# Moving fill units, first transposes and weight splits in a two-branch attention block

## The chip, the cores and the metric

The kernel runs on one core of a Trainium2 chip. The metric is device time in microseconds (us), as the median of several executions. The profile is of one further execution. TensorE is PE in the rows, VectorE DVE, ScalarE ACT, GpSimd POOL, SyncE SP.

## What is computed

One decoder block for 512 tokens of width 1024, in float32. All that matters here is this, cut from the reference:

```python
h = rms_norm(x, norm_g[layer])
proj = h @ w_in[layer]
fq, fk, fv, fz, mq, mk, mv, mz, ga, gb, fl = split_cols(proj, IN_SPLITS)
# fox: 8 heads of 64, causal, with a forget bias; q and k are RMS-normalised
y_fox = from_heads(fox_attention(q, k, v, log_f)) * jax.nn.silu(fz)
# moba: 8 heads of 64; q and k are RMS-normalised and rotated (partial_rope)
y_moba = from_heads(moba_attention(q, k, v)) * jax.nn.silu(mz)
merged = (jax.nn.sigmoid(ga + b_gate[layer, 0]) * (y_fox @ w_fox[layer])
          + jax.nn.sigmoid(gb + b_gate[layer, 1]) * (y_moba @ w_moba[layer]))
x = x + merged @ w_out[layer]
```

At 512 tokens and blocks of 256, every block is selected, so moba is computed as causal attention as well.

## The kernel before

**Precision.** A float32 operand is split in a high part (a ScalarE copy) and a low part (a VectorE subtraction), and a product is three matmuls: high by high, high by low, low by high. A weight chunk is 128 x 4 x 256 numbers; `split` (L131 to L137) makes its two parts, named wh and wl, with four buffers each.

**Fill units.** A name such as fkb is 256 columns of the input projection: branch f or m, then q, k, v or z, then half a or b. Its weights come in two chunks. `unit(name, t)` computes 128 tokens of it, 24 matmuls into a bank of the tag pj (two banks), and evicts it. For q and k each second unit normalises two token tiles: a square sq on ScalarE, a reduction on VectorE, a power and a product on GpSimd, and for branch m four rotation steps on GpSimd (`norm_qk`, `do_rope`). sq has the tag u, which it shares with ysh. v is split in two parts and kept. The units of wf0 to wf3 multiply fox's result by w_fox; the target of the first eviction, f03, has the tag v with two buffers, and so comes after v_mva.

**Attention groups.** There are four groups: fox a, fox b, moba a, moba b, of four heads each. A group consists of steps. Tr(0), Tr(1) transpose q and k of a pair of heads into p_qT and p_kT, split them, and copy KH to the other 64 partitions by a DMA. Aa(h) computes logits lg and exponentials. Bb(h) transposes the exponentials through three banks p_a, p_b, p_cc, splits them (pth, ptl) and multiplies by v into the only bank pv; ScalarE copies half of it (ysh) and VectorE adds. Yp(pair) scales. p_qT, p_kT, p_a, p_b, p_cc and p_ri share the tag tp with three banks. A group's body is Aa(0), Aa(1), Tr(1), Bb(0), Aa(2), Bb(1), Yp(0), Aa(3), with the previous group's Yp(1) put behind Aa(0); its tail is Bb(2), Bb(3). Tr(0) of the next group is the step `following`.

**Order.** `inter` (L1023) deals the steps of a group and the units of its fill alternately into one program order, in proportion to their numbers. The fill of group 0 is fkb, fqb, fvb, of group 1 mka, mqa, mva, of group 2 mkb, mqb, mvb, of group 3 wf0 to wf3. From the program order a planner makes a fixed order for each engine ahead of the run: by its own estimates of time it issues, on each engine, the instruction that is ready and stands earliest in program order. So TensorE's matmuls of steps and of units are mixed finely, and a unit can run far ahead of its place. Buffers of one tag are given out in program order.

**Splits.** Every fill unit first calls `pump(i)` (L179): it makes the splits up to piece i + 3 and, as raw buffers come free (four), has SP load further chunks. i is the first piece of the unit's own name (two less for wf), so the first unit of a name has both pieces of the next name split. In the first two groups two units of each fill also carry `make_sums`, six VectorE instructions and two ScalarE copies, with stores.

Of the kernel before, what the change touches and what calls it, by code (L numbers as in the profile page):

```python
# [25 lines left out]
C_NG, C_BG, C_FQ, C_FK, C_MQ, C_MK, C_BF, C_GQ, C_GK, C_END = 0, 8, 24, 25, 26, 27, 28, 36, 52, 68  # L26
# [3 lines left out]
def fox_moba_kernel(ctx: ExitStack, tc, xT, x, w_in, w_fl, w_fox, w_moba, w_out, cst, rope, out):  # L30
# [3 lines left out]
    V, A, G, T = nc.vector, nc.scalar, nc.gpsimd, nc.tensor  # L34
# [56 lines left out]
    def col(c, n=1):  # L91
        return cs[:, c:c + n]
# [13 lines left out]
    for i in range(WARM):  # L106
# [8 lines left out]
                    fill=NEG, base=0, channel_multiplier=1)  # L115
# [60 lines left out]
    loads, preps, first_prep = [], [], {}  # L176
    done = {"loads": 0, "preps": 0}

    def pump(i):  # L179

        while True:
            j = done["loads"]
            if j < len(loads) and (j < WR or loads[j - WR][1] < done["preps"]):
                loads[j][0]()
                done["loads"] += 1
            elif done["preps"] < len(preps) and done["preps"] <= i + 3:
                preps[done["preps"]]()
                done["preps"] += 1
            else:
                return  # L190
# [65 lines left out]
    def make_sums(k):  # L256
        def tl(tag, dt=F32):
            return t2("y", 15, f"sum_{tag}", dt=dt)
        a, b = XT[k], XT[k + 4]
        out = []  # L260
        f0, f1 = tl("sf"), tl("sf")
        s3, s2, s1, s4 = f0[:, 0:HT], f0[:, HT:S], f1[:, 0:HT], f1[:, HT:S]
        for o, x, y, op in ((s3, a[:, 0:HT], a[:, HT:S], OP.subtract), (s1, a[:, HT:S], b[:, HT:S], OP.add),
                            (s2, s1, a[:, 0:HT], OP.subtract), (s4, b[:, 0:HT], s2, OP.subtract)):
            V.tensor_tensor(out=o, in0=x, in1=y, op=op)
        for i, f in enumerate((f0, f1)):
            hl = [tl("sh", F32R), tl("sl", F32R)]
            A.activation(hl[0], f, AF.Copy)
            V.tensor_tensor(out=hl[1], in0=f, in1=hl[0].bitcast(F32), op=OP.subtract)
            out.extend((d[2 * i:2 * i + 2, :, k, :].rearrange("s p t -> p s t"),  # L270
                        t.bitcast(F32).rearrange("p (s t) -> p s t", t=HT)) for d, t in zip(S_dram, hl))

        def store():
            for d, t in out:
                A.dma_start(out=d, in_=t)
        return store
# [71 lines left out]
    def rope_tables():  # L348
        nc.sync.dma_start(out=rp, in_=rope)
        for nm, c in (("mq", C_GQ), ("mk", C_GK)):  # L350
            tab = con.tile([P, NT, 32], F32, name=f"tab_{nm}")
            g = col(c, 16)
            G.tensor_tensor(out=tab[:, :, 0:16], in0=rp[:, :, 0:16],
                            in1=g[:, None, :].to_broadcast([P, NT, 16]), op=OP.mult)
            G.tensor_tensor(out=tab[:, :, 16:24], in0=rp[:, :, 16:24],
                            in1=g[:, None, 8:16].to_broadcast([P, NT, 8]), op=OP.mult)
            G.tensor_tensor(out=tab[:, :, 24:32], in0=rp[:, :, 24:32],
                            in1=g[:, None, 0:8].to_broadcast([P, NT, 8]), op=OP.mult)
            CA[nm] = tab
# [27 lines left out]
    def unit(name, t):  # L387
        def go():
            p = pj(f"pj_{name}{t}")
            unit_mm(p, name, t)  # L390
            if name[1] == "v":
                evac_v(p, name, t)
            else:
                evac_qk(p, name, t)
        return go
# [17 lines left out]
    def unit_z(name, c):  # L413
        def go():
            p = (tp if name == "fzb" else pj)(f"pz_{name}{c}")
            tr_mm(p, name, c)
            z = t2("y", 15, f"zs_{name}{c}")
            s = t2("u", 4, "sg")
            V.tensor_tensor(out=z, in0=p, in1=rbc, op=OP.mult)
            A.activation(s, z, AF.Tanh, scale=0.5)  # L420
            V.scalar_tensor_tensor(z, s, 1.0, z, op0=OP.add, op1=OP.mult)
            ZS["f", 2 * (name[2] == "b") + c] = z
        return go
# [67 lines left out]
    def moba_begin():  # L491
        for o in range(2):
            rows = slice(HD, HD + 32) if o == 0 else slice(0, 32)
            for tl in KLt[o]:
                G.memset(tl[rows, :].bitcast(F32), 0.0)
# [178 lines left out]
    def unit_f(i, c):  # L674
        def go():
            j = 2 * i + c
            p = pj(f"pf{j}")
            br_mm(p, f"wf{i}", "f", c)
            if j == 0:
                f = sb.tile([P, 4, S], F32, name="f03", tag="v", bufs=2)  # L680
                FS[0], FS[1] = f[:, 0:2, :], f[:, 2:4, :]
            elif j in (4, 6):
                FS[j // 2] = sb.tile([P, 2, S], F32, name=f"f{j}", tag="qk", bufs=4)
            A.activation(FS[i][:, c, :], p, AF.Copy)  # L684
        return go
# [134 lines left out]
    def merge_a(i, c):  # L820
        if True:
            j = 2 * i + c
            p = pj(f"pm{j}")
            br_mm(p, f"wm{i}", "m", c)
            u = SG[i][:, c, :]
            V.tensor_tensor(out=u, in0=p, in1=u, op=OP.mult)
            if i % 2:
                V.tensor_tensor(out=u, in0=u, in1=FS[i][:, c, :], op=OP.add)
            else:
                G.dma_start(out=u, in_=FS[i][:, c, :], accum_op=OP.add)  # L830
# [166 lines left out]
    def units(name):  # L997
        k = name[:2]
        if k[0] == "G":
            return groups[name]  # L1000
        if k == "wf":
            return [unit_f(int(name[2]), c) for c in range(2)]
        if k == "wm":
            i = int(name[2])
            return [lambda c=c: merge_a(i, c) for c in range(2)]
        if k[1] == "z":
            return [unit_z(name, c) for c in range(2)]
        return [unit(name, t) for t in range(4)]

    def filler(names):  # L1010
        res = []
        for nm in names:
            for n, u in enumerate(units(nm)):
                def go(i=first_prep[nm] + (n if nm[0] == "G" else -2 if nm[:2] == "wf" else 0), u=u):
                    pump(i)
                    u()
                res.append(go)
        return res

    def last_on(engine):  # L1020
        return next(i for i in reversed(nc.cur_bb.bb.instructions) if i.engine == engine)

    def inter(a, b):  # L1023
        n, m = len(a), len(b)
        ia = ib = 0
        while ia < n or ib < m:
            if ib >= m or (ia < n and ia * m <= ib * n):
                a[ia]()
                ia += 1
            else:  # L1030
                b[ib]()
                ib += 1

    def seq(names):
        for u in filler(names):
            u()
# [14 lines left out]
    norm_row()  # L1051
    pump(0)
    fz = filler(["fza", "fzb"])
    for k, u in enumerate(fz):
        u()
        if k < 3:
# [3 lines left out]
    enter("attention")  # L1060
    zero_kl()
    rope_tables()
    plan = (("f", "a", C_FQ, C_FK, ["fkb", "fqb", "fvb"]),
            ("f", "b", C_FQ, C_FK, ["mka", "mqa", "mva"]),
            ("m", "a", C_MQ, C_MK, ["mkb", "mqb", "mvb"]),
            ("m", "b", C_MQ, C_MK, ["wf0", "wf1", "wf2", "wf3"]))
    head, body, tail, gate = attn_group("f", "a", col(C_FQ), col(C_FK))
    head[0]()
    for n in range(4):
        nxt = []  # L1070

        def following(n=n, nxt=nxt):
            br, half, cq, ck = plan[n + 1][:4]
            if n == 1:
                moba_begin()
            nxt.extend(attn_group(br, half, col(cq), col(ck)))
            nxt[0][0]()
        fill = filler(plan[n][4])
        if n < 2:
            for k, at in ((2 * n, 2), (2 * n + 1, 6)):  # L1080
                store = []

                def with_sums(u=fill[at], k=k, store=store):
                    u()
                    with tc.issue_after(last_on(mybir.EngineType.DVE)):
                        store.append(make_sums(k))

                def with_store(u=fill[at + 1], store=store):
                    u()
                    store[0]()  # L1090
                fill[at], fill[at + 1] = with_sums, with_store
        inter(body + ([following] if n < 3 else []) + tail, fill)
        if n < 3:
            body, tail = nxt[1][:1] + gate + nxt[1][1:], nxt[2]
            gate = nxt[3]
# [138 lines left out]
```

## Time and profile before

| What | Value |
|---|---|
| median of 3 runs | 431.78 us (431.44 to 433.05) |
| profiled execution | 433.64 us |
| its span | 431.9 us |
| mean granted clock of its span | 0.994 |
| TensorE busy | 419.5 us |
| VectorE busy | 337.5 us |

A row of a timeline gives the start in us from the start of the span, the duration, the engine, the line, the operation, output and inputs, and the count; in brackets stands the time for which the engine had been idle before it, and what ended that. Ends of matmuls are modelled, so the starts are the better measure of TensorE's pace. In the table by stretch, PEclk is the granted clock of TensorE as a share of full speed.

### The profile page before, as it was taken

How to read it: one execution, taken by the hardware profiler on the slowest of the kernel's cores; microseconds unless marked ns; L12 is line 12 of the kernel's file. 1: busy time of each engine (PE TensorE's matmuls, PEld its weight loads, DVE VectorE, ACT ScalarE, POOL GpSimd, SP SyncE). 2: the span in 40 equal slices, each digit the busy share in tenths (PEclk: the TensorE clock that was granted, in tenths of full speed). 3: DMA queues.
4: the chain of work that ended last, by engine and by line, in shares of the span. 5: the costliest groups of instructions: out<-in, count | busy, mean ns of one | idle time of the engine just before them, and what ended most of it. 6: DMA issues, size and time to landing. Idle time of an engine off the chain costs nothing.

```text
span 431.9 us, 7832 instructions
## 1 busy us (share of the span) xinstructions
PE 419.5 (97%) x2956; PEld 391.5 (91%) x2956; DVE 337.5 (78%) x571; ACT 272.4 (63%) x521; POOL 111.2 (26%) x127
## 2 busy tenths in 40 slices
PE   7999999999989989999997999999999999999996
PEld 6998899999989979999985789999999989988884
DVE  4669976887959978697669766599998685789973
ACT  4985436867658575697657766437757534686450
POOL 1048200224204766018630105044000011022140
PEclk9999999999999999999999999999999999999999
DMA  7981235253452444331231104915050835796484
GB/s 241 396 293 58 69 127 150 68 187 118 129 145 87 129 130 137 122 123 40 95 106 43 26 24 179 361 71 178 21 194 2 271 71 116 239 261 116 98 142 152
DMA packets 26374, 59.53 MB, mean 138 GB/s; under 512 B 3168, under 2 KB 7968, under 8 KB 26336
## 3 DMA queue, kind: packets, MB, share of 16 engines
q1 hardware_dynamic: 13552, 38.38, 26.8%
q0 software_dynamic: 3968, 9.44, 9.9%
q10 hardware_dynamic: 8816, 11.21, 8.7%
q8 instruction: 23, 0.38, 0.4%
q14 instruction: 15, 0.12, 0.1%
HBM read 48.37 MB, written 6.32 MB: 127 GB/s over the span
## 4 chain that ended last, share of the span: by engine, by line
PE 59%; DVE 6%; issue 1%; DMA 1%; ACT 1%; ACTq 0%; DVEq 0%
PE pb_GB L748 3%; PE pb_GA L748 3%; PE pb_GA L745 3%; PE pb_GB L747 3%; PE pb_GB L745 3%; PE pb_GA L747 3%; PE po L948 3%; PE po L946 3%; PE po L947 3%; PE pm L671 2%; PE pm L672 2%; PE pm L670 2%; PE pf L670 2%; PE pb_GZ L747 2%; PE pb_GZ L748 2%; PE pb_GZ L745 2%
## 5 line engine op out<-in xcount | busy, mean ns | idle before, releaser
L334 POOL TENSOR_TENSOR ff<-ss,mh 128x8 f32<-128x8 f32 x16 | 30.5, 1914 | 59.8 <-DVE ss L332 59.4
L564 ACT ACTIVATE p<-p,negm 128x128 f32<-128x128 f32 (+1 forms) x64 | 35.7, 560 | 14.8 <-DVE negm L562 12.2
L562 DVE CUSTOM_DVE_ANT_0 p<-lg,mask 128x128 f32<-128x128 f32 (+1 forms) x64 | 30.9, 488 | 14.8 <-PE lg L560 14.1
L134 ACT ACTIVATE wh_GB<-wr_gb 128x1024 fp32r<-128x1024 f32 x14 | 14.6, 1058 | 13.9 <-PE pm L671 5.9
L559 PE MATMUL lg<-KH,QS 128*128 128x128 f32 (+1 forms) x64 | 20.8, 334 | 2.2 <-DMA KH<-KH 2.1
L136 DVE TENSOR_TENSOR wl_GA<-wr_ga,wh_GA 128x1024 fp32r<-128x1024 f32 x14 | 19.9, 1445 | 1.6 <-ACT wh_GA L134 1.6
L908 ACT ACTIVATE wh_o<-wr_o 128x1024 fp32r<-128x1024 f32 x14 | 14.8, 1058 | 10.0 <-PE pb_GB L747 2.8
L136 DVE TENSOR_TENSOR wl_GB<-wr_gb,wh_GB 128x1024 fp32r<-128x1024 f32 x14 | 16.8, 1218 | 5.0 <-ACT wh_GB L134 5.0
L909 DVE TENSOR_TENSOR wl_o<-wr_o,wh_o 128x1024 fp32r<-128x1024 f32 x14 | 16.9, 1220 | 3.7 <-ACT wh_o L908 3.7
L134 ACT ACTIVATE wh_GA<-wr_ga 128x1024 fp32r<-128x1024 f32 x14 | 14.4, 1055 | 6.5 <-DVE wr_ga L706 3.4
L830 POOL DMA_DIRECT2D uGB<-f x4 | 3.5, 870 | 56.9 <-issue 47.0
L638 ACT ACTIVATE ysh<-pv 64x512 f32<-64x512 f32 x16 | 9.5, 592 | 11.3 <-PE pv L614 8.9
L532 ACT ACTIVATE QS<-p_qT,cs 64x512 fp32r<-64x512 f32 x16 | 10.9, 682 | 7.6 <-PE p_qT L523 4.0
L559 PEld LDWEIGHTS lg<-KH,QS 128*128 128x128 f32 x64 | 12.0, 189 | 3.4 <-DMA KH<-KH 2.6
L533 DVE SCALAR_TENSOR_TENSOR QS<-p_qT,cs,QS 64x512 fp32r<-64x512 f32 x16 | 12.0, 750 | 3.2 <-ACT QS L532 2.8
L670 PE MATMUL pf<-yhf,wh_wf 128*128 128x512 f32 x32 | 13.0, 407 | 0.8 <-ACT f L684 0.8
L748 PE MATMUL pb_GA<-Gh,wl_GA 128*128 128x256 f32 x48 | 13.5, 281 | 0.0
L748 PE MATMUL pb_GB<-Gh,wl_GB 128*128 128x256 f32 x48 | 13.5, 281 | 0.0
L747 PE MATMUL pb_GA<-Gl,wh_GA 128*128 128x256 f32 x48 | 13.5, 281 | 0.0
L745 PE MATMUL pb_GA<-Gh,wh_GA 128*128 128x256 f32 x48 | 13.5, 281 | 0.0
L609 ACT ACTIVATE pth<-p_a 128x512 fp32r<-128x512 f32 x16 | 9.5, 593 | 6.3 <-PE p_a L603 6.2
L745 PE MATMUL pb_GB<-Gh,wh_GB 128*128 128x256 f32 x48 | 13.5, 280 | 0.0
(485 smaller groups left out, 1840.8 us busy)
## 6 DMA issues: line engine op xcount, KB each, us to landing
wr_ga<-in_w_in_dram SPq DMA_DIRECT2D x8, 512.0 KB, 6.4
wr_gb<-in_w_in_dram SPq DMA_DIRECT2D x8, 512.0 KB, 4.8
wr_o<-in_w_out_dram SPq DMA_DIRECT2D x8, 512.0 KB, 11.6
xt<-in_xT_dram SPq DMA_DIRECT2D x8, 256.0 KB, 5.9
x<-in_x_dram SPq DMA_DIRECT2D x8, 256.0 KB, 6.7
KH<-KH ACTq DMA_DIRECT2D x16, 128.0 KB, 2.3
s_dramh<-sum_sh ACTq DMA_DIRECT2D x8, 256.0 KB
s_draml<-sum_sl ACTq DMA_DIRECT2D x8, 256.0 KB, 3.3
```

The source lines that it names most:

```text
L134: A.activation(hi[:, :, 0:n], src, AF.Copy)
L136: eng.tensor_tensor(out=lo[:, q, 0:n], in0=src[:, q], in1=hi[:, q, 0:n].bitcast(F32), op=OP.subtract)
L334: G.tensor_tensor(out=f2, in0=ss.rearrange("p t h -> p (t h)"), in1=mh, op=OP.pow)
L559: T.matmul(lg[:, :n], qs[:, qt], kh[:, :n], start=True, stop=False)
L562: V.tensor_tensor_reduce(pt, lg[:, :n], mask[:, 512 - n:512], -0.125, 3.0e38, op0=OP.add, op1=OP.min, accum_out=mkn[:, hh, i:i + 1])
L564: A.activation(pt, pt, AF.Exp, bias=mkn[:, hh, i:i + 1], scale=-1.0, accum_out=rs[:, hh, i:i + 1])
L670: T.matmul(p, hi[:, k, cc], yh, start=(k == 0), stop=False)
L745: T.matmul(o, hi[:, k, cc], lh, start=(n < 3 and c == 0 and k == 0), stop=False, skip_group_check=True)
L747: T.matmul(o, hi[:, k, cc], ll, start=False, stop=False, skip_group_check=True)
L748: T.matmul(o, lo[:, k, cc], lh, start=False, stop=(k == 3), skip_group_check=True)
L908: A.activation(wide(hi), wide(R[key, c]), AF.Copy)
L909: V.tensor_tensor(out=wide(lo), in0=wide(R[key, c]), in1=wide(hi).bitcast(F32), op=OP.subtract)
```

## The change

Three edits. The first two units of a q, k or v name call `pump` with a number lower by one, so that the first piece of the next name is split at the first unit and the second at the third; this takes in fva, ahead of the groups. The last two units of v (":23") go to the head of the next group's fill, ahead of its other units. Tr(0) of the next group stands behind Bb(2) instead of before it.

With the new counts `inter` deals as follows. Group 0: ..., Aa(3), fqb3, Bb(2), fvb0, Tr(0), fvb1, Bb(3). Groups 1 and 2: ..., Aa(3), q2, Bb(2), q3, Tr(0), v0, Bb(3), v1, where q3 is the last unit of mqa or mqb. Before, it was ..., q3, Aa(3), v0, Tr(0), v1, Bb(2), v2, Bb(3), v3 in all three. Group 3 has ten units instead of eight.

```diff
+    def ahead(nm, n):
+        return n if nm[0] == "G" else -2 if nm[:2] == "wf" else -1 if nm[1] in "qkv" and n < 2 else 0
+
     def filler(names):
         res = []
         for nm in names:
+            nm, _, part = nm.partition(":")
             for n, u in enumerate(units(nm)):
-                def go(i=first_prep[nm] + (n if nm[0] == "G" else -2 if nm[:2] == "wf" else 0), u=u):
+                def go(i=first_prep[nm] + ahead(nm, n), u=u):
                     pump(i)
                     u()
-                res.append(go)
+                if not part or str(n) in part:
+                    res.append(go)
         return res
...
-    plan = (("f", "a", C_FQ, C_FK, ["fkb", "fqb", "fvb"]),
-            ("f", "b", C_FQ, C_FK, ["mka", "mqa", "mva"]),
-            ("m", "a", C_MQ, C_MK, ["mkb", "mqb", "mvb"]),
-            ("m", "b", C_MQ, C_MK, ["wf0", "wf1", "wf2", "wf3"]))
+    plan = (("f", "a", C_FQ, C_FK, ["fkb", "fqb", "fvb:01"]),
+            ("f", "b", C_FQ, C_FK, ["fvb:23", "mka", "mqa", "mva:01"]),
+            ("m", "a", C_MQ, C_MK, ["mva:23", "mkb", "mqb", "mvb:01"]),
+            ("m", "b", C_MQ, C_MK, ["mvb:23", "wf0", "wf1", "wf2", "wf3"]))
...
-        inter(body + ([following] if n < 3 else []) + tail, fill)
+        inter(body + tail[:1] + ([following] if n < 3 else []) + tail[1:], fill)
```

## Rows read from the trace of the kernel before

**Rows 1.** The page's share table: busy us (share of the span) and instructions of each engine.

```profile
PE 419.5 (97%) x2956; PEld 391.5 (91%) x2956; DVE 337.5 (78%) x571; ACT 272.4 (63%) x521; POOL 111.2 (26%) x127
```

**Rows 2.** Busy time by stretch, core 0; columns in the first line, clock where PEclk stands.

```profile
core 0: us, PE busy (x) PEld busy (x) DVE busy (x) ACT busy (x) POOL busy (x), PEclk, DMA share, GB/s
120.00:135.00 15.00, 13.70 (x112) 13.18 (x111) 10.20 (x22) 9.59 (x22) 1.82 (x2) 1.00 0.44 115
150.00:165.00 15.00, 13.11 (x93) 12.67 (x92) 11.84 (x27) 10.10 (x24) 7.27 (x8) 0.89 0.46 138
...
225.00:240.00 15.00, 12.15 (x67) 9.46 (x66) 13.85 (x31) 12.29 (x29) 0.00 (x0) 1.00 0.25 71
268.00:432.00 164.00, 159.75 (x1093) 147.72 (x1091) 131.30 (x145) 90.95 (x128) 25.80 (x23) 0.99 0.55 155
```

**Rows 3.** Waits of PE: engine line waited for: us, times, longest.

```profile
PE pv L614 <- DVE ptl L610: 2.5, 2, 1.9
PE lg L559 <- DMA KH<-KH: 2.1, 2, 1.3
```

**Rows 4.** Timeline of PE, 157 to 161: start us, us, operation, idle before in brackets.

```profile
157.80 0.33 PE L613 MATMUL pv<-pth,v_fvb 128*128 128x384 f32 x1
160.02 0.55 PE L614 MATMUL pv<-ptl,v_fvb 128*128 128x384 f32 x1 [1.89 <-DVE ptl L610]
```

**Rows 5.** Timeline of DVE, 156 to 160: the two splits ahead of ptl.

```profile
156.41 1.21 DVE L136 TENSOR_TENSOR wl_mkb<-wr_mkb,wh_mkb 128x1024 fp32r<-128x1024 f32 x1
...
158.16 1.21 DVE L136 TENSOR_TENSOR wl_mkb<-wr_mkb,wh_mkb 128x1024 fp32r<-128x1024 f32 x1
159.29 0.68 DVE L610 TENSOR_TENSOR ptl<-p_b,pth 128x512 fp32r<-128x512 f32 x1
```

**Rows 6.** Timeline of PE, 214 to 224, transposes alone (matmuls between them left out).

```profile
214.09 0.38 PE L523 MATMUL p_qT<-ident,qn_mqb 128*128 128x128 f32 x2
...
214.75 0.60 PE L603 MATMUL p_a<-ident,p 128*128 128x128 f32 x4
...
219.21 0.60 PE L603 MATMUL p_b<-ident,p 128*128 128x128 f32 x4
...
223.24 0.38 PE L523 MATMUL p_qT<-ident,qn_mqb 128*128 128x128 f32 x2
...
223.63 0.38 PE L603 MATMUL p_cc<-ident,p 128*128 128x128 f32 x2
```

**Rows 7.** Timeline of PE, 227 to 239: the end of the third group's last head.

```profile
228.28 0.33 PE L559 MATMUL lg<-KH,QS 128*128 128x128 f32 x1 [0.75 <-DMA KH<-KH]
...
228.85 0.60 PE L603 MATMUL p_a<-ident,p 128*128 128x128 f32 x4
...
235.67 0.37 PE L614 MATMUL pv<-ptl,v_mva 128*128 128x256 f32 x1
...
238.06 0.50 PE L670 MATMUL pf<-yhf,wh_wf 128*128 128x512 f32 x1 [0.76 <-ACT f L684]
```

**Rows 8.** Timeline of ACT, 212 to 238: the square, the KH copy, the branch's eviction.

```profile
212.29 0.59 ACT L638 ACTIVATE ysh<-pv 64x512 f32<-64x512 f32 x1 [0.79 <-PE pv L614]
212.91 0.63 ACT L327 ACTIVATE sq<-qn_mqb 128x512 f32<-128x512 f32 x1
...
224.95 0.49 ACTq L536 DMA_DIRECT2D KH<-KH  x1
...
237.41 1.09 ACT L684 ACTIVATE f<-pf 128x512 f32<-128x512 f32 x2
```

**Rows 9.** Timeline of POOL, 215 to 220: last of the normalising and rotation of mqb.

```profile
219.03 0.46 POOL L372 TENSOR_TENSOR qn_mqb<-ra,rb 128x128 f32<-128x128 f32 x1
```

**Rows 10.** Timeline of PE, 99 to 102: first and last of eighteen projection matmuls.

```profile
99.09 0.28 PE L306 MATMUL pj_fvb<-wh_fvb,Gh 128*128 128x256 f32 x1
...
101.07 0.28 PE L308 MATMUL pj_fvb<-wh_fvb,Gl 128*128 128x256 f32 x1
```

**Rows 11.** Timeline of DVE, 212 to 214: the sum that frees the pv bank.

```profile
212.91 0.69 DVE L639 TENSOR_TENSOR yma<-pv,ysh 64x512 f32<-64x512 f32 x1 [1.18 <-ACT ysh L638]
```

## The prediction, as it was made

> **What bounds the kernel now.** I read the page's share table first: TensorE is busy 97% of the span, no other engine over 78% [rows 1]. So only TensorE's own gaps can be won. Then the table by stretch, for where they lie [rows 2]. From 268 us to the end 159.75 of 164 us are busy and what is missing lies after the last product, out of the change's reach. In the attention stage, three stretches of 15 us are short: 120 to 135 by 1.30 us, 150 to 165 by 1.89, 225 to 240 by 2.85. In 150 to 165 the granted clock is 0.89 as well; with its two levels 2.4 and 1.2 GHz that is 2 x 0.11 x 15 = 3.3 us at the lower one, of which half, 1.65 us, is lost. In the other two it is 1.00. The idle counts come short by what the modelled ends hide: at 157.80 a 384-column matmul is followed by the next start only 2.22 us later, while the row itself puts the idle at 1.89 [rows 4]; less some 0.18 us of issue for 384 columns (an estimate: the 18 projection matmuls of 256 columns start 0.1165 us apart [rows 10], times 1.5) 2.04 us are lost, 0.15 more per restart.
>
> Three different causes, then:
>
> - A, at 124 us: PE waits 1.30 us for the copy of KH [rows 3].
> - B, at 158 us: PE waits 1.89 us for ptl [rows 3, 4]. On VectorE two splits of one weight name, wl_mkb, 1.21 us each, were queued ahead of it, at 156.41 and 158.16 [rows 5].
> - C, 225 to 240 us: several short waits, 2.85 us. The row behind the last shows why there was no filler: pf waits for the eviction of an earlier pf [rows 7], which runs only at 237.41 [rows 8]. Its target f03 has the tag of the v tiles, so it needs the buffer of v_mva, and v_mva's last product stands at 235.67 [rows 7]. Two banks pj were full until then.
>
> Why was v_mva held so long? The transposes p_qT and p_kT of the next group take two of three tp banks at 214.09 and wait for the second half of q, which POOL finishes at 219.03 + 0.46 = 219.5 [rows 6, 9]; the second half of p_qT is at 223.24 [rows 6]. Head 2 has one bank in that time: p_a at 214.75, p_b at 219.21, p_cc at 223.63 [rows 6]. Head 3 begins at 228.85 [rows 7].
>
> **The change, part by part.** No instruction is added or removed. The fill units keep their order among themselves; what moves is their place against the attention steps, the order of Tr(0) and Bb(2), and the place of the splits with the loads that follow them on SP's queue.
>
> *Tr(0) behind Bb(2).* In program order Bb(2) now asks for its three tp banks first. One-bank working passes on to Bb(3), which then runs while the second half of q is normalised, where before it began behind Tr(0). The last product of v_mva, before at 235.67, can then come about when Tr(0) ends; at 223 to 230 (an estimate: the second p_qT at 223.24 plus up to the 6.8 us that head 3 took before, 235.67 - 228.85 [rows 6, 7]). f03 comes free 5 us or more earlier and pf goes on. Of C that leaves the wait for KH, 0.75 [rows 7]. C by starts is 2.85 + 5 x 0.15 = 3.6; less 0.75 + 0.15 = 0.9 for KH, **2.7 us** are won. Bounds: 0 (head 3 is no earlier) and 3.6.
>
> *v's last two units into the next fill.* Each unit has 24 matmuls, 24 x 0.1165 = 2.8 us [rows 10]. At the head of groups 1 to 3 that is 5.6 us of filler that needs nothing of the attention. But TensorE took filler whenever attention was not ready, and would have run these units in the same gaps; the total is the same. I give it nothing by itself: it is the supply on which the 2.7 rests. In the first group the fill is shorter by 5.6 us, and wait A stands at its end; the next units stand ready behind them as before. A: 0, bounds -1.45 to +1.45.
>
> *Splits one piece at a time.* pump stands one piece lower for the first two units of q, k and v names. Of two 1.21 us splits in a row one comes two units later. At B that takes one from in front of ptl: **1.2 us** won. What is late next there is ptl itself behind one split; 0.8 us of idle would stay. The cover: a piece has still two units, 5.6 us, until the unit that reads it, against 1.1 us of copy and 1.2 us of subtraction; if VectorE were later than that, each missing piece costs up to its 1.21. The loads on SP go with the pieces, one by one instead of in pairs; nothing waits there for weights in this stage, so 0. On ACT and VectorE the second piece of a name and one set of sums of the first group now come in one unit; both are off the path while PE has filler, bounds 0 to 1.2.
>
> *The clock after B.* The low clock followed the idle of 1.89 us [rows 4]; idles of 1.30 and of 0.75 to 2.85 in pieces left it at 1.00 [rows 2]. With 0.8 left it should not fall: 1.65 won in this execution. But its time of 433.64 is 1.86 over the median of 431.78, about the price of one fall, so the other runs may not have it. I take **0.8**, bounds 0 and 1.65. The Trainium skill (TensorE: Matmul & The Clock Gate, A second HAM failure mode: psum-queue depth-cycling) says that many micro-idles from cycling PSUM banks can make the clock oscillate too. C is such a stretch, and this trace does not agree: granted 1.00 over it [rows 2]. By the page C would be worth some microseconds more; the sum goes by the row.
>
> *The new cost.* In groups 1 and 2 the twelve steps alternate with twelve units, and Tr(0) now comes straight after the last q unit, which itself stands behind Bb(2). Its square sq shares a tag with ysh; buffers go in program order, and the trace has sq at 212.91 right behind the ysh of head 1 at 212.29 [rows 8]. After the change it waits for the ysh of head 2. That head needs the pv bank, free at 212.91 + 0.69 = 213.6 [rows 11], then some 1.2 us of products (8 matmuls, 2048 columns at the pitch of rows 10, rounded up) and 0.59 of ysh: sq at 215.4, 2.5 us later. q is then ready at 222.0 instead of 219.5, still before the 223.24 at which TensorE took it up. So 0 if TensorE takes it at once, 2.5 at each of two boundaries if the same 3.75 us pass again and no filler is there. I take **1.0** in all, nearest to the 0.75 and 1.30 us that KH's waits cost now [rows 3, 7]; bounds 0 and 5.
>
> Sum: -2.7 - 1.2 - 0.8 + 1.0 = -3.7 us. The profiled execution has 433.64 (span 431.9 and 1.74 around it) and would come to 429.9; on the median, 431.78 - 3.7 = **428.1**.
>
> **The rivals.** (1) All three gaps go: A 1.45, B 2.04 and 1.65, C 3.6, together 8.7: 423.0. For it: loads in single pieces no longer crowd the copy of KH. Against it: A's wait is for a DMA and nothing moves that copy itself. (2) No difference. The order on each engine is fixed ahead by the planner's estimates, and every one of the gaps is a place where the chip was later than it; a new order has new such places. Three new waits of 1.3 us against the 3.7 give about 431.8. For it: A and B are of this kind; against it: C has its cause in the order of the banks. (3) Slower: the chain sq, power, rotation, Tr(0), KH, moved behind head 2's ysh, ends last at the boundaries of groups 1 and 2. Each then has the 2.5 us and, as behind B, 1.65 us of low clock: 4.15. At the second, filler ends at pf as before and C stays, so only B's 2.0 are won: 431.78 + 8.3 - 2.0 = 438; with one boundary alone 434. It decides once q's second half is ready after the filler in hand is used up: some 2.5 units of mvb and two of pf at 212 us, 12.6 us, against 10 to 14 us to the first lg. For it: that margin is thin; against it: Bb(3) and Aa's own work fill as well.
>
> **How the numbers follow.** The likeliest, 424.5 to 429.6: 0.45. Rival 1, below 424.5: 0.12. Rival 2, within 0.5% (429.6 to 433.9; about what a measurement of this kernel can tell from no change): 0.25. Rival 3: 0.18, half of it at 435 or less. Faster 0.57, same 0.25, slower 0.18. The range 423.0 to 435.0 leaves out about half of rival 3 and half of rival 1. Cases of both signs lie in it; the likeliest one's own range is 424.5 to 429.6.
>
> **What would show it.** In the profile after: p_a, p_b and p_cc of head 2 ahead of p_qT and close together; v_mva's last product before 231 us and the eviction f03 soon behind; one wl_mkb, not two, ahead of head 3's ptl, the clock at 1.00 in the whole stage; no wait of PE over 1.5 us from 60 to 270 us. Wrong if sq stands behind head 2's ysh and PE waits for p_qT or KH at the boundaries, if VectorE's later pieces leave PE waiting for wl, or if new waits appear elsewhere in the stage of the sum of those that went.

## The result and the profile after

The change makes the kernel slower.

| | before | changed |
|---|---|---|
| median | 431.95 us (431.44 to 433.05, 4 runs) | 436.82 us (435.89 to 438.47, 4 runs) |
| ratio, 95% interval | | 1.0117 (1.0081 to 1.0152) |
| profiled execution, its span | 433.64, 431.9 us | 436.07, 434.3 us |

The two profiled executions differ by 2.4 us only, the medians by 4.9: that of before stands 1.7 above its median, that of the changed kernel 0.75 below. The traces can thus show about half of the loss.

The share table of the changed kernel, as [rows 1]:

```profile
PE 419.4 (97%) x2956; PEld 389.5 (90%) x2956; DVE 333.7 (77%) x571; ACT 272.2 (63%) x521; POOL 112.3 (26%) x127
```

Busy time by stretch, as [rows 2] (us, busy and number by engine, granted clock, DMA):

```profile
core 0: us, PE busy (x) PEld busy (x) DVE busy (x) ACT busy (x) POOL busy (x), PEclk, DMA share, GB/s
120.00:135.00 15.00, 12.71 (x104) 12.32 (x103) 9.05 (x22) 8.65 (x20) 0.52 (x1) 1.00 0.40 87
150.00:165.00 15.00, 15.00 (x122) 14.69 (x121) 12.60 (x29) 10.93 (x27) 8.55 (x10) 1.00 0.57 166
225.00:240.00 15.00, 12.85 (x56) 9.77 (x55) 10.84 (x20) 9.48 (x21) 1.61 (x2) 0.89 0.08 18
255.00:270.00 15.00, 12.82 (x91) 11.00 (x91) 12.07 (x28) 12.19 (x31) 3.17 (x5) 1.00 0.31 103
270.00:285.00 15.00, 13.52 (x112) 13.23 (x110) 7.49 (x10) 5.54 (x8) 3.87 (x6) 1.00 0.94 354
```

Stretch B (150 to 165) is mended: TensorE is busy throughout, at full clock. A has grown, 15 - 12.71 = 2.29 us idle instead of 1.30. C is little better, 2.15 us idle instead of 2.85, and now the clock falls there (0.89). And two stretches are short, 255 to 270 by 2.2 us and 270 to 285 by 1.5, that were whole in the kernel before:

```profile
255.00:270.00 15.00, 15.00 (x99) 13.62 (x98) 11.61 (x20) 10.16 (x23) 5.76 (x9) 1.00 0.36 131
270.00:285.00 15.00, 15.00 (x128) 15.00 (x127) 9.23 (x11) 6.58 (x10) 1.29 (x1) 1.00 0.85 309
```

So the idle time moved rather than went. From 60 us to the last product of the attention TensorE is idle 6.0 us before and 6.6 us now, behind it 4.2 and 5.7 us.

The longest waits of TensorE, as [rows 3]; lg for KH are A and part of C:

```profile
PE lg L559 <- DMA KH<-KH: 3.2, 2, 2.3
...
PE pb_GZ L747 <- DMA S0l<-s_draml: 1.5, 1, 1.5
PE pv L613 <- DVE ymb L639: 1.0, 1, 1.0
PE p_cc L603 <- DVE ptl L610: 0.9, 1, 0.9
```

The chain at the head of the fourth group, as [rows 8]: ScalarE's square of q's second half, KH's copy, the eviction to f03 (timeline of ACT).

```profile
217.19 0.60 ACT L638 ACTIVATE ysh<-pv 64x512 f32<-64x512 f32 x1 [1.06 <-PE pv L614]
217.69 0.62 ACT L327 ACTIVATE sq<-qn_mqb 128x512 f32<-128x512 f32 x1
...
227.12 0.48 ACTq L536 DMA_DIRECT2D KH<-KH  x1
...
231.20 1.09 ACT L684 ACTIVATE f<-pf 128x512 f32<-128x512 f32 x2
```

GpSimd's part of that chain, as [rows 9]: the power, the product, the last rotation step.

```profile
219.89 2.63 POOL L334 TENSOR_TENSOR ff<-ss,mh 128x8 f32<-128x8 f32 x1
222.61 1.05 POOL L336 TENSOR_TENSOR qn_mqb<-qn_mqb,ff 128x512 f32<-128x512 f32 x1
...
224.84 0.47 POOL L372 TENSOR_TENSOR qn_mqb<-ra,rb 128x128 f32<-128x128 f32 x1
```

And TensorE, as [rows 6, 7]: the second half of p_qT, the fourth group's first lg, the last product with v_mva.

```profile
225.36 0.44 PE L523 MATMUL p_qT<-ident,qn_mqb 128*128 128x128 f32 x2
...
229.45 0.47 PE L559 MATMUL lg<-KH,QS 128*128 128x128 f32 x2 [0.92 <-DMA KH<-KH]
...
230.17 0.38 PE L614 MATMUL pv<-ptl,v_mva 128*128 128x256 f32 x1
```

The square follows head 2's ysh at once; from it to the end of the rotation (224.84 + 0.47) are 7.6 us, p_qT starts within 0.1 us of that, KH's copy leaves at 227.12, and lg starts at 229.45, 1.2 us later than before. v_mva is done at 230.17 instead of 235.67, and f03 is evicted at 231.20 instead of 237.41, as forecast. It bought nothing. The following rows show where the time went instead. First the timelines of the kernel before for GpSimd and TensorE near 262 us: the scaling Yp(0) of the fourth group, the second of the loads of the sums S, which stand behind it on GpSimd's queue, the last matmul of the fill, and the last product of the attention.

```profile
261.75 1.30 POOL L655 TENSOR_TENSOR ymb<-ymb,rinv_bc 128x512 f32<-128x512 f32 x1 [20.37 <-DVE ymb L639]
...
263.77 0.55 POOL L282 DMA_DIRECT2D S0l<-s_draml  x1
```

```profile
262.77 0.39 PE L672 MATMUL pf<-yhf,wl_wf 128*128 128x512 f32 x1
...
272.33 0.28 PE L614 MATMUL pv<-ptl,v_mvb 128*128 128x256 f32 x1
```

Now the changed kernel: the same two matmuls (timeline of PE), and the chain of work that ended last, 264 to 276 us (start, us, what).

```profile
253.15 0.39 PE L672 MATMUL pf<-yhf,wl_wf 128*128 128x512 f32 x1
...
272.95 0.28 PE L614 MATMUL pv<-ptl,v_mvb 128*128 128x256 f32 x1
```

```profile
266.83 0.66 POOL ymb L655
...
268.09 0.75 POOL S0h L282
268.84 5.94 DMA S0l<-s_draml
...
274.82 0.38 PE pb_GZ L747
```

The fill is used up 9.6 us earlier (253.15 against 262.77). Products of the next part, pb_GZ, fill in until 258.7; from there to 268.8 the fourth group's steps stand alone on TensorE. Yp(0) is 5.1 us later (266.83 against 261.75), the load of S0l with it (268.84 against 263.77), and the first product that reads S0l waits for that load until 274.82. The last product of the attention itself is only 0.6 us later (272.95 against 272.33). So of the 2.4 us that the trace shows, 1.8 stand behind the attention.

### The profile page after: what moved, and what is told of

Its sections match the earlier page's. It is cut to its first block, busy times and chain, and to the rows that moved or that the text cites. A ratio compares the mean times of both kernels' runs of the same rounds, so it can differ in the third digit from the quotient of the medians.

```text
span 434.3 us, 7838 instructions
## 1 busy us (share of the span) xinstructions
PE 419.4 (97%) x2956; PEld 389.5 (90%) x2956; DVE 333.7 (77%) x571; ACT 272.2 (63%) x521; POOL 112.3 (26%) x127
## 4 chain that ended last, share of the span: by engine, by line
PE 73%; DMA 9%; DVE 7%; ACT 4%; POOL 3%; issue 2%; SPq 1%; ACTq 0%; DVEq 0%; POOLq 0%
PE pb_GB L748 3%; PE pb_GA L748 3%; PE pb_GA L747 3%; PE pb_GB L745 3%; PE pb_GA L745 3%; PE pb_GB L747 3%; PE po L948 3%; PE po L946 3%; PE po L947 3%; PE lg L560 2%; PE lg L559 2%; DMA KH<-KH 2%; PE pm L671 2%; PE pm L670 2%; PE pm L672 2%
## 5 line engine op out<-in xcount | busy, mean ns | idle before, releaser
L334 POOL TENSOR_TENSOR ff<-ss,mh 128x8 f32<-128x8 f32 x16 | 29.1, 1822 | 68.2 <-DVE ss L332 50.2
L610 DVE TENSOR_TENSOR ptl<-p_a,pth 128x512 fp32r<-128x512 f32 x16 | 11.0, 686 | 8.4 <-ACT pth L609 7.4
```

Of the source, the lines that this page charges most:

```text
L334: G.tensor_tensor(out=f2, in0=ss.rearrange("p t h -> p (t h)"), in1=mh, op=OP.pow)
```

## Experiments

The ratios are to the kernel before on the same chip. The table has, from the timelines, the start of the square of mqb's second half, the fourth group's first lg, the last product with v_mvb (the end of the attention), and the span of the profiled execution.

| Kernel | square | first lg | last product | span | median | ratio (95%) |
|---|---|---|---|---|---|---|
| before | 212.9 | 228.3 | 272.3 | 431.9 | 431.95 | 1 |
| changed | 217.7 | 229.4 | 272.9 | 434.3 | 436.82 | 1.0117 (1.0081 to 1.0152) |
| pieces_alone | 212.1 | 228.8 | 272.2 | 431.9 | 432.42 | 0.999 (0.9969 to 1.0011) |
| tr_later_alone | 212.2 | 229.2 | 272.0 | 434.0 | 437.43 | 1.0106 (1.0076 to 1.0136) |
| units_and_tr_later | 218.3 | 230.2 | 273.9 | 438.0 | 439.12 | 1.0141 (1.0111 to 1.0171) |
| pieces_and_tr_later | 205.9 | 222.3 | 265.5 | 427.4 | 429.12 | 0.9922 (0.9895 to 0.9948) |
| q3_before_head2 | 217.1 | 237.3 | 279.6 | 439.2 | 439.62 | 1.0141 (1.0103 to 1.0178) |
| changed_three_u | 217.2 | 229.1 | 272.6 | 434.6 | 437.25 | 1.0104 (1.0076 to 1.0132) |
| changed_own_square | 206.6 | 222.8 | 268.2 | 427.9 | 430.14 | 0.9923 (0.9898 to 0.9948) |
| before_own_square | 204.3 | 221.9 | 270.9 | 432.0 | 432.3 | 0.9974 (0.9958 to 0.999) |
| tr_later_own_square | 203.3 | 222.0 | 267.5 | 429.0 | 431.94 | 0.997 (0.9947 to 0.9994) |
| pieces_tr_own_square | 203.4 | 222.0 | 266.4 | 426.3 | 428.06 | 0.9873 (0.985 to 0.9895) |

A span is thus the start of the fourth group, the time from there to the last product, and the rest. The rest (span less last product) is 159.6 to 159.9 us in the five kernels in which TensorE waits for no load of S: before, pieces_alone, q3_before_head2, changed_own_square and pieces_tr_own_square. In the other seven it waits 1.2 to 2.1 us for them, and the rest is 161.1 to 164.1 us.

v's move alone was not tried: with Tr(0) in its old place the last unit of q would stand behind the transposes that read it. Tr(0) one step later is what makes v's move possible.

**Theory L**, formed on the changed kernel's trace: the loss is the square that waits for head 2's ysh. The first kernels take the edits apart.

**pieces_alone**: the changed kernel with the plan and the order of before, `ahead()` kept.

```diff
-            ("m", "a", C_MQ, C_MK, ["mva:23", "mkb", "mqb", "mvb:01"]),
+            ("m", "a", C_MQ, C_MK, ["mkb", "mqb", "mvb"]),
...
-        inter(body + tail[:1] + ([following] if n < 3 else []) + tail[1:], fill)
+        inter(body + ([following] if n < 3 else []) + tail, fill)
```

> Only the splits are made a piece at a time; fills and Tr(0) stand as before. Theory L (the loss comes from the square of q's second half, which waits for head 2's ysh once two units of v lead the fill): this kernel has no late square, only wait B's second split is gone, so 1.2 to 3 us faster than before, 429 to 431 us. Theory P (the pieces come too late, or their loads crowd the copies): the loss is here already, 434 to 437 us.

432.42 us, ratio 0.999: no difference. Neither theory's number. The stretches A and B in its trace:

```profile
120.00:135.00 15.00, 12.55 (x89) 12.05 (x88) 7.23 (x20) 8.45 (x22) 1.80 (x2) 0.89 0.20 46
150.00:165.00 15.00, 13.59 (x111) 13.22 (x110) 14.75 (x31) 10.97 (x24) 10.96 (x14) 1.00 0.62 183
```

TensorE's waits for ptl are down from 2.5 to 0.6 us and the clock is whole at B, but 1.41 us are idle there for the rotation of mqa, and A has grown to 15 - 12.55 = 2.45 us, with the low clock now at A: what B gave, these waits took.

**tr_later_alone**: the kernel before with Tr(0) one step later.

```diff
-        inter(body + ([following] if n < 3 else []) + tail, fill)
+        inter(body + tail[:1] + ([following] if n < 3 else []) + tail[1:], fill)
```

> Only Tr(0) stands behind Bb(2); fills and splits as before, so the last unit of q is still ahead of Aa(3) and its square waits for head 1's ysh. Theory L: no loss, and the banks go to head 2 first, so wait C shrinks: 429 to 432 us, v_mva's last product before 233 us. Theory T (Tr(0) itself is late because it asks for its banks behind head 2): 434 to 437 us, with Tr(0) of the fourth group later than 225 us.

437.43 us: this edit alone has the size of the whole loss, though its square stands behind head 1's ysh as before. Theory L in its first form falls. Nor does its attention end late: by the table the last product stands at 272.0 against 272.3, and the 2.1 us by which the span is longer lie behind it (162.0 against 159.6), where TensorE waits 1.9 us for loads of S. Inside the attention GpSimd's timeline shows one long chain: power, product, a scaling of the fox branch (L651), and the four rotation steps of mqa's second half.

```profile
164.02 1.65 POOL L334 TENSOR_TENSOR ff<-ss,mh 128x8 f32<-128x8 f32 x1 [3.14 <-DVE ss L332]
...
166.90 1.30 POOL L651 TENSOR_TENSOR rinv_bc<-zs_fzb,rinv_bc 128x512 f32<-128x512 f32 x1
...
169.03 1.30 POOL L368 TENSOR_TENSOR rb<-qn_mqa,tab_mq 128x64 f32<-128x64 f32 x1
...
171.14 1.52 POOL L372 TENSOR_TENSOR qn_mqa<-ra,rb 128x128 f32<-128x128 f32 x1
```

VectorE beside it (timeline of DVE):

```profile
166.96 1.78 DVE L269 TENSOR_TENSOR sum_sl<-sum_sf,sum_sh 128x512 fp32r<-128x512 f32 x1
168.67 1.49 DVE L136 TENSOR_TENSOR wl_mqb<-wr_mqb,wh_mqb 128x1024 fp32r<-128x1024 f32 x1
...
171.14 1.21 DVE L136 TENSOR_TENSOR wl_mqb<-wr_mqb,wh_mqb 128x1024 fp32r<-128x1024 f32 x1
```

From the power to the last step are 8.6 us, and TensorE waits 1.70 us for the result at Tr(0) of the third group. In the kernel that wins, pieces_and_tr_later, the same seven operations but L651 run like this:

```profile
159.73 1.65 POOL L334 TENSOR_TENSOR ff<-ss,mh 128x8 f32<-128x8 f32 x1 [1.76 <-DVE ss L332]
...
163.00 0.32 POOL L368 TENSOR_TENSOR rb<-qn_mqa,tab_mq 128x64 f32<-128x64 f32 x1
...
163.68 0.46 POOL L372 TENSOR_TENSOR qn_mqa<-ra,rb 128x128 f32<-128x128 f32 x1
```

4.4 us. The stretched steps lie beside long VectorE operations, two of them the splits of wl_mqb. But this chain does not explain the loss. The kernel before, which does not lose, has stretched steps in the same place:

```profile
169.02 0.83 POOL L368 TENSOR_TENSOR rb<-qn_mqa,tab_mq 128x64 f32<-128x64 f32 x1
169.81 1.31 POOL L370 TENSOR_TENSOR rb<-qn_mqa,tab_mq 128x64 f32<-128x64 f32 x1
```

And in pieces_alone, which does not win, the same two steps take 0.33 us each.

**q3_before_head2**: the changed kernel with q's last unit ahead of head 2 again, in groups 2 and 3.

```diff
+        if n in (1, 2):
+            q3, bb2 = fill[9], tail[0]
+            def both():
+                q3()
+                bb2()
+            fill[9], tail = lambda: None, [both] + tail[1:]
         inter(body + tail[:1] + ([following] if n < 3 else []) + tail[1:], fill)
```

> The changed kernel with one exchange: in groups 1 and 2 the last unit of q is put ahead of Bb(2) instead of behind it, so that its square can take its buffer ahead of head 2's ysh. Theory L: the square of mqb's second half starts before head 2's ysh, q is ready about 5 us earlier (220 instead of 225.3), the fourth group starts at 225 to 227 instead of 229.5, and the waits at 260 to 275 us shrink: 430 to 433 us. Rivals (fill moved out of reach, late pieces): the square's place does not matter, 435 to 438 us.

439.62 us; the gain of theory L did not come. Timeline of ACT (the ysh is head 1's) and TensorE's waits:

```profile
216.49 0.59 ACT L638 ACTIVATE ysh<-pv 64x512 f32<-64x512 f32 x1
217.10 1.15 ACT L327 ACTIVATE sq<-qn_mqb 128x512 f32<-128x512 f32 x2
```

```profile
PE p_qT L523 <- POOL qn_mqb L372: 5.3, 1, 5.3
PE lg L559 <- DMA KH<-KH: 4.1, 2, 2.9
```

Both squares of mqb stand behind the same ysh of head 1, go together (x2), and GpSimd then has both halves one after the other, until 231.9 us by its timeline; TensorE waits 5.3 us for the first of them. So it isn't head 2 alone: a square waits for whichever ysh stands ahead of it in the shared tag, and the whole chain behind it counts.

**units_and_tr_later**: the changed kernel with the preparation due as before.

```diff
-        return n if nm[0] == "G" else -2 if nm[:2] == "wf" else -1 if nm[1] in "qkv" and n < 2 else 0
+        return n if nm[0] == "G" else -2 if nm[:2] == "wf" else 0
```

> The change without its third edit: two units of v lead the next fill and Tr(0) stands behind Bb(2), but both pieces are split at a name's first unit as before. Theory L: as slow as the changed kernel or slower by wait B's 1.2 to 3.8 us, 436 to 440 us. Theory P: the loss goes, 430 to 433 us.

439.12 us, in the range of theory L; the late pieces are not the cause.

**Theory S**: the end of the loss is in the loads of S. Three kernels issue them from SyncE.

```diff
-                nc.gpsimd.dma_start(out=t.bitcast(F32), in_=d[i])
+                nc.sync.dma_start(out=t.bitcast(F32), in_=d[i])
```

> The kernel before, with the loads of the sums S issued from SyncE. There TensorE waited for none of them. Theory S: no difference, 431.5 to 433.5 us; it is the control for the other two kernels with this edit. If it gains as much as they do, the loads are not what the change lost by.

> Only Tr(0) behind Bb(2), and the eight loads of the sums S are issued from SyncE instead of GpSimd, where they stand behind the scaling Yp(0) of the fourth group (265.16 us; S0l is waited for until 273.98). Theory S (the loss ends in these loads): the wait on S0l goes, 433.5 to 435.5 us instead of 437.4. Theory F (the fill is used up early and head 1 to 3 of the fourth group stand bare): the wait on S0l goes but TensorE waits elsewhere between 255 and 275 us, 436.5 to 438 us.

> The changed kernel with the loads of the sums S issued from SyncE. Theory S: the wait of 1.48 us on S0l goes, 433.5 to 435.5 us. Theory F: 436 to 438 us, with the waits of 260 to 269 us as they were.

440.05 us (1.0171), 438.55 (1.0131) and 437.58 (1.0135). The edit does not test the theory: SyncE's queue in before_s_on_sync, and TensorE's wait,

```profile
271.92 0.38 SPq L282 DMA_DIRECT2D S0h<-s_dramh  x1
...
277.05 0.32 SPq L282 DMA_DIRECT2D S3l<-s_draml  x1
```

```profile
PE pb_GZ L745 <- DMA S0h<-s_dramh: 4.8, 1, 4.8
```

show the loads 8 to 9 us later than from GpSimd, behind weight loads, and the wait for S0h, 4.8 us, is over half of the 8.6 us by which its span is longer. In the other two waits for S remain as well, 2.9 and 1.0 us. That these loads can cost is shown; whether the changed kernel would be whole without its 1.5 us is open.

**pieces_and_tr_later**: the changed kernel with the plan of before.

```diff
-    plan = (("f", "a", C_FQ, C_FK, ["fkb", "fqb", "fvb:01"]),
+    plan = (("f", "a", C_FQ, C_FK, ["fkb", "fqb", "fvb"]),
...
```

> Tr(0) behind Bb(2) and splits a piece at a time; fills as before. If the edits add (pieces alone 0.999, Tr(0) later alone 1.0106): 1.010, 436.5 to 438 us. If the changed kernel's loss needs v's two units in the next fill as well: 432 to 434.5 us.

429.12 us, 0.8% faster than before: below both expectations. The edits do not add: 0.999 and 1.0106 make 0.9922. Why the two edits gain together was not isolated. And v's two units, put on top of this, cost 1.0117 / 0.9922 = 1.0197, about 8.5 us. The table shows what goes with it: the fourth group starts at 222.3 instead of 228 to 230, and ends 43.2 us later. Over before, the four single and double edits, the changed kernel and q3_before_head2 that stretch is 42.3 to 44.0 us, whatever the fill: here the fill ends at 250.5, earlier still than in the changed kernel. The end of the stage follows the start of its last group.

**Theory L2**, from this: a group starts when q's second half is through square, power, product, rotation, Tr(0) and KH; the square waits for a ysh only since the two share the tag u; TensorE's filler hides this chain as long as it lasts. (In pieces_and_tr_later too the square, at 205.9, comes right behind head 1's ysh; there the whole third group is early.) Test: the square gets a tag of its own, and u one buffer less, so that the memory stays the same.

```diff
-        sq = t2("u", 4, "sq", (P, 2, CW))
+        sq = sb.tile([P, 2, CW], F32, name="sq", tag="sq", bufs=1)
...
-                sh = t2("u", 4, "ysh")
+                sh = t2("u", 3, "ysh")
```

> The changed kernel, with the square sq in a tag of its own with one buffer, and three instead of four buffers for the tag u that ysh keeps. Theory L2 (each group starts when q's second half is ready, that waits for a ysh because of the shared tag, and the fourth group then takes 43 us whatever fills it): mqb's second square comes well before the 217.7 us of the changed kernel, the fourth group's first lg before 226 us instead of 229.4, its last product 43 to 44 us later, and the time is 429 to 433 us. Rival E (the start of a group is set elsewhere, by KH's copy, VectorE or the planner's order): the square is early and the group starts at 228 us or later, 435 to 439 us.

> The kernel before, with the square in a tag of its own as above. Theory L2: its squares waited for the ysh of head 1, so its groups start earlier too: first lg of the fourth group before 226 us instead of 228.3, 427 to 431 us. Rival E: 431 to 434 us with the group's start at 228 us or later.

> Pieces and Tr(0) behind Bb(2), without v's move, with the square in a tag of its own. Theory L2: at least as fast as without it, 425 to 429.5 us, the fourth group's first lg at 222 us or before. Rival E: 429 to 434 us.

430.14, 432.3 and 428.06 us. The changed kernel gains some 1.9% (1.0117 to 0.9923), the kernel before 0.26%. In the changed kernel's trace (timelines of ACT and PE) the square of mqb stands free of head 2's ysh, 11 us earlier, and the fourth group's first lg 6.6 us earlier:

```profile
203.99 0.59 ACT L638 ACTIVATE ysh<-pv 64x512 f32<-64x512 f32 x1
...
206.58 0.64 ACT L327 ACTIVATE sq<-qn_mqb 128x512 f32<-128x512 f32 x1
...
209.40 0.59 ACT L638 ACTIVATE ysh<-pv 64x512 f32<-64x512 f32 x1 [1.59 <-PE pv L614]
```

```profile
222.82 0.22 PE L559 MATMUL lg<-KH,QS 128*128 128x128 f32 x1
```

This lead is older than the fourth group. By TensorE's timelines it is 10.1 us at the first lg of the second group (115.9 against 126.0) and 9.5 at that of the third (172.4 against 181.9). So the squares of the earlier groups make it, not that of mqb alone; no run frees one by itself.

By the table the group then lasts 268.2 - 222.8 = 45.4 and 266.4 - 222.0 = 44.4 us in the first and the third, a little above the 42 to 44 of the others, so most of the earlier start is kept. In before_own_square the group starts early as well, at 221.9, as theory L2 has it, but takes 49.0 us, not 43, and the 427 to 431 us did not come: the start is not the only bound. There the third group's last product, with v_mva, stands at 233.1, against 224.2 to 228.4 in the three others, so head 3 of the third group runs far into the fourth; that this is the bound is a reading that no run isolates. pieces_tr_own_square is the best version: 1.3% faster than before.

Two more kernels asked whether the smaller number of u buffers won, and whether tr_later_alone lost by the same cause.

> The changed kernel with three instead of four buffers for the tag u, and the square still in it. Theory L2 (it is the square's own tag that won in the changed kernel): the square of mqb's second half still follows a ysh at 215 us or later and the time is 435 to 440 us. Rival U (fewer u buffers only re-deal the order, and that won): 428 to 432 us, with the square early.

> Only Tr(0) behind Bb(2), fills and splits as before, with the square in a tag of its own. Theory L2: Tr(0) later alone lost because the chain from the square to Tr(0) still sets the start of a group, so with an early square the loss goes, 429 to 433 us, the fourth group's first lg before 226 us. Rival (Tr(0) behind Bb(2) loses by the banks or by the splits in pairs): 435 to 438 us.

437.25 us with three buffers and a shared square, which stands at 217.2 as in the changed kernel: it is the tag. 431.94 us for Tr(0) later with its own square, against 437.43: this loss too is there only while the square shares its tag (1.0106 with it, 0.997 against 0.9974 without). That its chain is later than in the kernel before isn't what the trace shows (square 212.2 against 212.9); how the sharing makes Tr(0)'s move cost stays open.

## Why the prediction was wrong

I forecast 428.1 us and 0.57 for faster. The chain of rival 3, to which I had given 0.18, carries the loss: with a square of its own the changed kernel doesn't lose. But the time does not go the way it was priced there, 2.5 us and a low clock at each of two boundaries. TensorE waits 0.9 us for KH at the second, with the low clock behind it, and not at all at the first; most of the traced loss stands behind the attention. And head 2's ysh is not needed for it: tr_later_alone loses as much with the square behind head 1's. That 436.82 lies between its prices of 434 and 438 is partly luck. Of the 4.9 us of the medians the traces show 2.4; where the others are stays open.

- *What bounds the kernel.* "Only TensorE's own gaps can be won" took each gap as a prize by itself. This is the step that failed first. The gaps moved: 6.0 us of idle time in the attention became 6.6. TensorE is busy with filler while the attention chain runs, and this chain sets the end of the stage: the first lg of the fourth group plus 42 to 44 us. The share of 97% hides this. And the part from 268 us on, said to be out of the change's reach, took 1.8 of the 2.4 us, 1.5 of them the wait for S0l.
- *Tr(0) behind Bb(2), -2.7.* The intermediate points came: three banks for head 2 (its last product at 216.73), v_mva at 230.17, 0.2 past the range 223 to 230, f03 at 231.20. The gain did not: C is still 2.15 us idle, now with a low clock. By itself the edit cost 1.06%.
- *v's units, "nothing by itself".* Wrong by the whole result: 8.5 us on top of the other two edits, 0.5% (0.9923 against 0.9873) where the square has its own tag. I saw the shift of q's last unit behind Bb(2) and charged it to the new cost.
- *The new cost, 1.0 within 0 to 5.* The right mechanism, mis-sized. I had the square at 215.4 and q ready at 222.0; the trace has 217.69 and 225.3. (The eight products of a head have 2 x 1280 = 2560 columns, not 2048; at the pitch of rows 10 that is 1.2 us all the same.) The larger error was the reference: I compared q's readiness with the 223.24 at which TensorE took it before, and held the rest hidden by filler. Undoing the shared tag measures the cost: 1.0117 to 0.9923, some 8 us, part of which the kernel before pays too (0.26%).
- *Splits in pieces, -1.2 and the clock -0.8.* At B it came true, with the clock at 1.00. By itself it gave nothing (0.999), since A grew and the low clock moved there. With Tr(0) later it gave 1.8% (1.0106 to 0.9922), for which I had no term and have no shown cause.
- *A, 0 within 1.45.* It grew by 1.0 us. I held that nothing moves this copy. But it stands at the head of the second group, behind the same chain: in the four kernels with a square of its own that group starts at 115.9 to 119.8 us, before at 125.7, and TensorE does not wait for KH at all. Why it grew in the changed kernel was not settled.
- *The rule on micro-idles* (the Trainium skill, TensorE: Matmul & The Clock Gate, A second HAM failure mode: psum-queue depth-cycling): before, C did not bear it out. In the changed kernel the clock does fall, once, in that stretch (0.50, its lower level, from 231 to 234 us), after a wait of 0.9 us of p_cc for ptl, which reads a bank of the same tag, and one of 0.9 us for KH's DMA. It costs 15 x (1 - 0.89) = 1.65 us. A fall behind short waits fits the Trainium skill, but no oscillation is seen, and no run tells the two waits apart.

## What to carry to other kernels

When a filler keeps the busiest engine full, time each group in the trace from its first step to the next group's first step, and cost an edit by what it does to the chain in between and to the loads that wait for the stage's end. If two unrelated temporaries share a tag whose buffers go out in program order, a change of order makes one wait for the other: give the one on the chain its own buffer before moving anything. Edits of an order do not add, so measure the pairs.

## What the runs showed of the hardware

GpSimd's elementwise steps were up to four times longer beside VectorE's operations on two SBUF inputs (spans on GpSimd are rough): the rotation step of 128x64 took 1.30 us and the sum of 128x128 1.52 beside the splits of wl_mqb in tr_later_alone, 0.32 and 0.46 us in pieces_and_tr_later. VectorE pays too: the subtraction at 166.96 took 1.78 us, where the same form takes 0.69 elsewhere. The Trainium skill (GPSIMD Engine Reference, Key points) says that the two engines share their SBUF interfaces and contend when VectorE's instruction has two SBUF inputs; these rows agree.
